# SSM phase tables in short fused instructions, and copies, modulation evictions and a GELU step moved between VectorE and ACT

## The chip, the cores and the metric

The kernel runs on one core of one Trainium2 chip. The metric is the device time of one execution in microseconds (us). The engines are named as in the profile: PE is TensorE (matmul, with its weight loads as PEld), DVE is VectorE, ACT is ScalarE, POOL is GpSimd, and SP only issues DMAs.

## What is computed

Two layers of a diffusion backbone over 512 latent tokens and 256 context tokens, model width 1024. Each layer mixes tokens in three parallel ways that share one input and one output projection, and then has a SwiGLU FFN. Norm and modulation come before each half.

```python
def modulate(x, shift, scale):
    return x * (1 + scale) + shift
...
    h = modulate(rmsnorm(x, g_pre_mix), sh1, sc1) @ w_in
...
    y_ssm, yc_ssm = s5_mixer(u, uc, ...)          # 24 groups, 64 complex states, two directions
    y_fft = fnet_mixer(f, w_fourier)
...
    y_na = na_latent(q, k, v, kc, vc, na_rpb)
    o = jnp.concatenate([y_ssm, y_fft, y_na], axis=-1) @ w_out
...
    x = x + g2 * rmsnorm(swiglu(modulate(rmsnorm(x, g_pre_ffn), sh2, sc2), ...), g_post_ffn)
```

In the S5 mixer the recurrence h = lam_bar * h + B u runs over the tokens, its output passes through a tanh GELU and a GLU. The kernel turns each complex state by a known phase, so that a real scan is left: it needs tables of cos and sin of 2 pi times n times a turn, for n = 0 to 95 steps of eight tokens.

## The kernel before

**Matmuls.** They take float32 split into a high and a low part (`split`, L579: an ACT copy that rounds, then a subtraction for the rest on DVE or POOL), three products each. `wsT` (L584, matmuls at L589) makes the projections `w_in` and gate/up, L1050 is `w_out`, L1146 the down projection.

**Stages.** For each layer: modulation and norm, `make_h` (L537), then `w_in` woven with `ssm` (12 units k: six quadruples of groups u times two directions d), `w_v`, attention woven with FNet and GLU, `w_out` with the second `make_h`, and the FFN, at whose end stands the `make_h` of the next layer. In layer 0 the tables of unit k+1 are made just ahead of their use (`prep_dir` with `jit`, which calls `phase`); those of layer 1 are made during the FFN of layer 0 (`prep`, which calls `phases` and `prep_dir` without `jit`) and loaded back by `tables`. A scheduler that simulates the timeline orders the instructions of each engine when the program is built, so an engine's order is not the order of the source; at run time every engine works its queue in that order.

**The touched places.** `phase` (L395) makes one unit's cos and sin table, 128 partitions x 4 groups x 96: on DVE a product with the turn (through the helper `tt`, L278), an addition of 12582912 that rounds (helper `ts`, L275), and a subtraction (helper `stt`, L281); on ACT Abs (L404) and two Sin (L405, L406). `prep_dir` (L431) makes a unit's matrices: three DVE products into `bm` (L278), three POOL products (L452 to L456), a cleared tile `b0` with 16 of every 32 columns copied (L460, L461), four PE transposes (L464) with an ACT eviction (L469), a small product on PE (L480) whose result DVE copies into `w` (L483, L486). `make_h` transposes the normed rows on PE (L552), evicts with scale and shift by DVE from PSUM (`f`, L275, out c, in b,am,mc) and splits `f` (ACT L580, DVE or POOL L561). `ssm_scan` (L703) has the DVE products, four DVE scans (L724) and the POOL rotation back (L727 to L737). `ssm_out` (L741) ends in the GELU: ACT Square (L758), a DVE `ts`, a DVE `tt`, ACT Tanh (L761), a DVE `stt`.

Of the kernel before, what the change touches and what calls it, by code (L numbers as in the profile page):

```python
# [8 lines left out]
F32 = mybir.dt.float32  # L9
F32R = mybir.dt.float32r  # L10
I32 = mybir.dt.int32
AF = mybir.ActivationFunctionType
ALU = mybir.AluOpType
# [16 lines left out]
TWO_PI = 6.2831845  # L30
# [4 lines left out]
class Builder:  # L35
    def __init__(self, tc, ctx, ap):
        self.tc, self.nc, self.ap = tc, tc.nc, ap
        pool = lambda name, bufs, **k: ctx.enter_context(tc.tile_pool(name=name, bufs=bufs, **k))
        self.ring_raw = pool("ring_raw", 2)
        self.ring_hi = pool("ring_hi", 4)  # L40
        self.ring_lo = pool("ring_lo", 4)
        self.tab_p = pool("tab", 3)
        self.x_p = pool("xp", 3)
        self.g_p = pool("gp", 2)
        self.u_p = pool("up", 1)
        self.s_p = pool("sp", 24)
        self.q_p = pool("qp", 12)
        self.c_p = pool("cp", 22)
        self.z_p = pool("zp", 2)
        self.sm_p = pool("sm", 18)  # L50
        self.ss_p = pool("ss", 12)
        self.am_p = pool("am", 24)
        self.b0_p = pool("b0p", 2)
        self.keep = pool("keep", 1)
        self.ps_p = {t: pool("ps_" + t, n, space=PSUM) for t, n in (("m", 3), ("a", 2), ("t", 2), ("o", 1))}
        self.dr_p = pool("dr", 1, space=DRAM)
# [39 lines left out]
    def consts(self):  # L96
        nc = self.nc
        self.cols = self.k("cols", [128, 8])
        nc.sync.dma_start(self.cols, self.ap["cols"])
        self.ident = self.k("ident", [128, 128])  # L100
        self.nidx = self.k("nidx", [128, 96])
        self.eye16 = self.k("eye16", [128, 16])
        self.junk = self.k("junk", [128, 512], mybir.dt.bfloat16)
        self.zero = self.k("zero", [1, 128], mybir.dt.bfloat16)
        nc.vector.memset(self.zero, 0.0)
        self.sgn, self.nsgn, self.sgn2pi, self.halfpi = (self.cols[:, i:i + 1] for i in range(4))
        self.mhalf = self.cols[:, 4:5]
        self.qd = [self.dram(f"qd{l}", [NH * HD, 2, NT]) for l in range(DEPTH)]
        self.kd = [self.dram(f"kd{l}", [NH * HD, 2, NT]) for l in range(DEPTH)]
        self.ud = [self.dram(f"ud{l}", [G, HC, 8, 128]) for l in range(DEPTH)]  # L110
        self.zd = [self.dram(f"zd{l}", [G, HC, 8, 96]) for l in range(DEPTH)]
        self.tabd = [self.dram(f"tabd{l}", [NU, 2, 128, 1792]) for l in range(DEPTH)]
        self.wd = [self.dram(f"wd{l}", [NU, 128, 240]) for l in range(DEPTH)]
        self.gd = [self.dram(f"gd{l}", [4, DM]) for l in range(DEPTH)]
        self.rbd = [self.dram(f"rbd{l}", [NH, 16, 8, 384]) for l in range(DEPTH)]
        self.xd = [self.dram(f"xd{l}", [6, 128, DM]) for l in range(3)]
        self.turn = [self.k(f"turn{l}", [128, 48]) for l in range(DEPTH)]
        self.rho = [self.k(f"rho{l}", [128, 48]) for l in range(DEPTH)]
        self.mcol = [[self.k(f"mc{l}{a}", [128, 2, 16]) for a in range(3)] for l in range(DEPTH)]
        self.gcol = [self.k(f"gcol{l}", [128, 2, 8]) for l in range(DEPTH)]  # L120
        self.amod = [[self.k(f"am{l}{i}", [128, 2, 8]) for i in range(2)] for l in range(DEPTH)]
        self.dcol = [self.k(f"dcol{l}", [128, NU]) for l in range(DEPTH)]

    def consts_load(self):
        nc = self.nc
        nc.sync.dma_start(self.ident, self.ap["ident"])
        nc.sync.dma_start(self.nidx, self.ap["nidx"])
        nc.sync.dma_start(self.eye16, self.ap["eye16"])
        for l in range(DEPTH):
            nc.sync.dma_start(self.gcol[l], self.ap["gpre"][l])  # L130
            nc.sync.dma_start(self.dcol[l], self.ap["ssm_d"][l])
# [263 lines left out]
    def phase(self, l, u, d, dst):  # L395

        o = (u * 2 + d) * 4
        sh = [128, 4, 96]
        cs, sn = (dst[:, i:i + 384].rearrange("p (g n) -> p g n", g=4) for i in (0, 384))
        self.tt(sn, self.nidx.unsqueeze(1).to_broadcast(sh), self.turn[l][:, o:o + 4].unsqueeze(2).to_broadcast(sh),  # L400
                ALU.mult)
        self.ts(cs, sn, 12582912.0, ALU.add)
        self.stt(sn, cs, -12582912.0, sn, ALU.add, ALU.subtract)
        self.nc.scalar.activation(cs, sn, AF.Abs)  # L404
        self.nc.scalar.activation(cs, cs, AF.Sin, scale=-TWO_PI, bias=self.halfpi)  # L405
        self.nc.scalar.activation(sn, sn, AF.Sin, scale=self.sgn2pi)  # L406

    def phases(self, l, u):

# [20 lines left out]
    def prep_dir(self, l, fin, k, jit, tags):  # L430

        nc = self.nc
        u, d = k // 2, k % 2
        if d == 0:
            self.prep_load(l, u)
        bc, w = self.bc, self.w
        o = k * 4
# [8 lines left out]
        bm, bt = xb[:, 0], xb[:, 1]  # L446
# [4 lines left out]
        g = nc.gpsimd  # L451
# [4 lines left out]
        g.tensor_tensor(out=cl, in0=cl, in1=ct, op=ALU.add)  # L456
        e0 = 1 if d == 0 else 0
        clv = cl[:, :, e0:e0 + 8, :].rearrange("p g e h -> p g (e h)")
        b0 = self.b0_p.tile([128, 4, 32], F32, tag="b0", name="b0")
        nc.vector.memset(b0, 0.0)  # L460
        nc.vector.tensor_copy(b0[:, :, 0:16], bm[:, :, 0 if d == 0 else 7, :])  # L461
        tp = self.ps(tags[0], [128, 4, 128])
        for i in range(4):
            nc.tensor.transpose(tp[:, i, :], bm[:, i].rearrange("p e h -> p (e h)"), self.ident)  # L464
# [13 lines left out]
        kp = self.ps(tags[1], [128, 128])  # L478
# [1 line left out]
            nc.tensor.matmul(kp[32 * i:32 * i + 32, :], b0[:, i, :],  # L480
                             cl[:, i, 1 - e0:9 - e0, :].rearrange("p e h -> p (e h)"), start=True, stop=True)
        if d == 0:
            nc.vector.tensor_copy(w[:, 112:240], kp)  # L483
            self.stt(w[:, 112:128], self.eye16, self.dcol[l][:, u:u + 1], w[:, 112:128], ALU.mult, ALU.add)
        else:
            nc.vector.tensor_copy(w[:, 0:112], kp[:, 0:112])  # L486
            self.tt(w[:, 112:128], w[:, 112:128], kp[:, 112:128], ALU.add)
            nc.sync.dma_start(self.wd[l][u], w)
            if jit:
                res.append(self.toeplitz(l, u))  # L490
# [47 lines left out]
    def make_h(self, l, i, xn, t0, ks=range(8)):  # L538

        nc = self.nc  # L540
# [8 lines left out]
        for k in ks:  # L549
# [2 lines left out]
                nc.tensor.transpose(tp[:, j, :], xn[j][k // 4][:, k % 4 * 128:(k % 4 + 1) * 128], self.ident)  # L552
            a, s = self.amod[l][i][:, v, k:k + 1], self.modB(l, i, v, k)
            f = self.c()
            self.ts(f, tp.rearrange("p j c -> p (j c)"), a, ALU.mult, s, ALU.add)
            ins = self.split(self.hh[k][v][:, cs], self.hl[k][v][:, cs], f, nc.gpsimd if k % 2 else nc.vector)
            if t0 == 0:
                self.h_ins = ins
# [181 lines left out]
    def ssm_out(self, l, k, tab, hh):  # L740
# [14 lines left out]
            self.z = self.z_p.tile([128, 8, 96], F32, tag="z", name="z")  # L755
        z = self.z
        w3 = self.q(shape=(128, 4, 96))
        nc.scalar.activation(w3, yp, AF.Square)  # L758
        self.ts(w3, w3, 0.044715, ALU.mult, 1.0, ALU.add)
        self.tt(w3, w3, yp, ALU.mult)  # L760
        nc.scalar.activation(w3, w3, AF.Tanh, scale=0.7978845608028654)  # L761
        o = (u % 2) * 4
        self.stt(z[:, o:o + 4, :], w3, 1.0, yp, ALU.add, ALU.mult)
# [545 lines left out]
def _consts():  # L1309
    f = np.float32  # L1310
    c = {}
    c["ident"] = np.eye(128, dtype=f)
    sg = np.where(np.arange(128) < 64, 1.0, -1.0)
    cols = np.zeros((128, 8))
    cols[:, 0], cols[:, 1], cols[:, 2], cols[:, 3], cols[:, 4] = sg, -sg, sg * TWO_PI, np.pi / 2, -0.5
    c["cols"] = cols.astype(f)
    c["nidx"] = np.broadcast_to(np.arange(96, dtype=f), (128, 96)).copy()
    p = np.arange(128)
# [94 lines left out]
```

## Time and profile before

| what | value |
|---|---|
| three runs, median (lowest to highest) | 1692.61 us (1690.66 to 1693.28) |
| the profiled execution, its own time | 1691.85 us |
| its span, first to last instruction | 1690.1 us |
| mean granted TensorE clock | 0.978 of full speed |
| busy: PE / DVE / ACT / POOL | 1613.3 / 1038.1 / 611.8 / 381.3 us |
| DMA | 242.96 MB, mean 144 GB/s |

Busy time of an engine is the time in which at least one of its instructions runs; an instruction that is held up by another engine counts as busy. A window row gives this by stretch. A group row gives the mean of one instruction, and after the bar the idle time of the engine before the group and what ended it.

### The profile page before, as it was taken

Reading aid. Unit: us, or ns where it says so; the run is one execution under the profiler, and the core shown is the slowest. Engines: PE = TensorE matmul, PEld = TensorE weight load, DVE = VectorE, ACT = ScalarE, POOL = GpSimd, SP = SyncE. Lnnn points to the kernel's source line nnn. Section 1 sums busy time; section 2 is a strip of 40 time slices with the busy share of each in tenths; the row PEclk is TensorE's granted clock in tenths of the full one; section 3 lists DMA queues with packets and bytes.
Section 4 is the critical chain, followed back from the end, with each engine's and each line's share of the span. In section 5 each row is a group of like instructions: output and inputs, shape, how many; then the busy total and the mean of one; then the engine's idle time right before and its main releaser. Section 6 shows DMA issues by size and latency. Waiting matters only on the chain. (4 is left out here: it accounts for less than half of the span.)

```text
span 1690.1 us, 23611 instructions
## 1 busy us (share of the span) xinstructions
PE 1613.3 (95%) x9121; PEld 1320.7 (78%) x9121; DVE 1038.1 (61%) x1893; ACT 611.8 (36%) x1091; POOL 381.3 (23%) x384
## 2 busy tenths in 40 slices
PE   5987789999999999999999999999999999999997
PEld 1776676678898888878878787988877888888886
DVE  7799984675774657534433348698773634454455
ACT  5433344572636522212211126421563532222222
POOL 3367673200320224100000005267410200000002
PEclk8999799999999999999999999999999999999999
DMA  9343338652403433544242527478714422222222
GB/s 327 126 133 115 113 101 278 213 214 102 169 32 119 165 116 118 181 156 150 103 155 105 203 84 241 133 242 248 228 45 143 157 100 100 75 100 100 100 75 87
DMA packets 101681, 242.96 MB, mean 144 GB/s; under 512 B 25457, under 2 KB 56817, under 8 KB 88257
## 3 DMA queue, kind: packets, MB, share of 16 engines
q1 hardware_dynamic: 98256, 232.80, 40.4%
q0 software_dynamic: 3312, 8.65, 1.7%
q8 instruction: 72, 1.18, 0.3%
q14 instruction: 41, 0.33, 0.1%
HBM read 204.12 MB, written 38.47 MB: 144 GB/s over the span
## 5 line engine op out<-in xcount | busy, mean ns | idle before, releaser
L589 PE MATMUL b<-s,wh 128*128 128x512 f32 (+1 forms) x1856 | 553.0, 376 | 1.7 <-DVE s L561 1.3
L589 PEld LDWEIGHTS b<-s,wh 128*128 128x128 f32 x1856 | 339.6, 190 | 73.9 <-issue 10.6
L589 PE MATMUL b<-s,wl 128*128 128x512 f32 (+1 forms) x928 | 346.6, 375 | 1.9 <-DVE wl L561 1.9
L580 ACT ACTIVATE wh<-wr 128x1024 fp32r<-128x1024 f32 (+1 forms) x188 | 190.3, 1034 | 334.2 <-PE b L589 232.1
L561 DVE TENSOR_TENSOR wl<-wr,wh 128x1024 fp32r<-128x1024 f32 (+1 forms) x188 | 231.8, 1247 | 108.8 <-ACT wh L580 103.4
L278 DVE TENSOR_TENSOR q<-q,b 128x512 f32<-128x512 f32 (+1 forms) x192 | 129.2, 676 | 165.8 <-PE b L1146 165.1
L589 PEld LDWEIGHTS b<-s,wl 128*128 128x128 f32 x928 | 175.7, 190 | 32.5 <-DVE wl L561 3.0
L589 PE MATMUL b<-c,wh 128*128 128x256 f32 x944 | 184.8, 290 | 0.0
L589 PEld LDWEIGHTS b<-c,wh 128*128 128x128 f32 x944 | 155.7, 196 | 5.9 <-issue 0.6
L281 DVE SCALAR_TENSOR_TENSOR s<-s,b 128x512 f32<-128x512 f32 x88 | 60.2, 684 | 132.9 <-PE b L589 83.8
L1146 PE MATMUL b<-wh,tab 128*128 128x512 f32 x400 | 137.2, 393 | 0.7 <-DVE q L278 0.7
L589 PE MATMUL b<-c,wl 128*128 128x256 f32 x472 | 135.2, 289 | 0.0
L1146 PE MATMUL b<-wh,s 128*128 128x512 f32 x384 | 129.6, 391 | 0.0
L1178 POOL TENSOR_TENSOR q<-q,g 128x512 f32<-128x512 f32 x10 | 13.8, 1382 | 360.6 <-ACT junk L515 360.6
L589 PEld LDWEIGHTS b<-c,wl 128*128 128x128 f32 x472 | 92.8, 197 | 1.7 <-issue 0.4
L1146 PEld LDWEIGHTS b<-wh,tab 128*128 128x128 f32 x400 | 75.1, 188 | 20.0 <-ACT c L1123 2.5
L1146 PEld LDWEIGHTS b<-wh,s 128*128 128x128 f32 x384 | 72.1, 188 | 20.0 <-issue 2.5
L1146 PE MATMUL b<-wl,tab 128*128 128x512 f32 x200 | 78.3, 392 | 0.0
L527 POOL TENSOR_TENSOR ss<-ss,cols 128x1 f32<-128x1 f32 x42 | 31.0, 737 | 194.1 <-DVE ss L281 193.4
L1146 PE MATMUL b<-wl,s 128*128 128x512 f32 x192 | 74.6, 390 | 0.0
L452 POOL TENSOR_TENSOR u<-x,u 128x576 f32<-128x576 f32 x24 | 31.5, 1311 | 168.8 <-PE b L480 143.3
L580 ACT ACTIVATE s<-s 128x512 fp32r<-128x512 f32 x36 | 22.6, 627 | 113.6 <-DVE s L281 58.4
(301 smaller groups left out, 2761.7 us busy)
## 6 DMA issues: line engine op xcount, KB each, us to landing
wr<-in_w_gu SPq DMA_DIRECT2D x44, 1024.0 KB
wmod<-in_w_mod SPq DMA_DIRECT2D x46, 512.0 KB
wr<-in_w_down SPq DMA_DIRECT2D x22, 1024.0 KB
wmod<-in_w_mod SPq DMA_DIRECT2D x16, 1024.0 KB
wr<-in_w_in SPq DMA_DIRECT2D x10, 1024.0 KB
u<-in_w_mod SPq DMA_DIRECT2D x18, 512.0 KB
wr<-in_w_out SPq DMA_DIRECT2D x8, 1024.0 KB
tab<-tabd SPq DMA_DIRECT2D x12, 640.0 KB
```

Of the source, the lines that this page charges most:

```text
L278: self.nc.vector.tensor_tensor(out=out, in0=a, in1=b, op=op)
L281: self.nc.vector.scalar_tensor_tensor(out=out, in0=a, scalar=s, in1=b, op0=op0, op1=op1)
L452: g.tensor_tensor(out=cl, in0=v(2).unsqueeze(2).to_broadcast(sc), in1=clr.unsqueeze(3).to_broadcast(sc), op=ALU.mult)
L527: nc.gpsimd.tensor_tensor(out=ss[:, 3:4], in0=ss[:, 2:3], in1=self.mhalf, op=ALU.pow)
L561: (eng or self.nc.vector).tensor_tensor(out=lo, in0=x, in1=hi.bitcast(F32), op=ALU.subtract)
L580: ins = self.nc.scalar.activation(hi, x, AF.Copy)
L589: self.nc.tensor.matmul(out, a[k], h[k][v][:, cs], start=(k == 0 and i == 0), stop=(k == 7 and i == 2))
L1146: nc.tensor.matmul(pd, a[v][:, cs], w[:, ds], start=(j == 0 and i == 0), stop=(j == n - 1 and i == 2))
L1178: (nc.gpsimd, nc.vector)[hf].tensor_tensor(out=oo[hf], in0=oo[hf], in1=gates[t // 4][:, hf * 512:(hf + 1) * 512], op=ALU.mult)
```

## The change

`phase`: the three DVE instructions of 384 columns become four fused `ts` of 96 columns (index times turn plus 12582912, the turn as a per-partition operand), an ACT pass that takes 12582912 off again (Identity with a bias column), and four `stt` of 96 columns (index times turn minus the rounded value). The sign of the result is reversed, so the sine takes the reversed scale column. `phases`, used for layer 1, stays as it is.

`prep_dir`: `b0` becomes two lasting tiles, cleared once by POOL at the start; the copy into it and the copies of the small product go from DVE to ACT.

`make_h`: the eviction `f` goes from DVE to ACT, with scale and shift as per-partition operands.

`ssm_out`: the factor 0.044715 goes into the Square's scale, and `ts` and `tt` become one `stt`.

```diff
+        self.b0 = [self.k(f"b0{i}", [128, 4, 32]) for i in range(2)]
...
-        self.mhalf = self.cols[:, 4:5]
+        self.mhalf, self.nsgn2pi, self.nmagic = (self.cols[:, i:i + 1] for i in range(4, 7))
...
+        for b0 in self.b0:
+            nc.gpsimd.memset(b0, 0.0)
...
-        sh = [128, 4, 96]
         cs, sn = (dst[:, i:i + 384].rearrange("p (g n) -> p g n", g=4) for i in (0, 384))
-        self.tt(sn, self.nidx.unsqueeze(1).to_broadcast(sh), self.turn[l][:, o:o + 4].unsqueeze(2).to_broadcast(sh),
-                ALU.mult)
-        self.ts(cs, sn, 12582912.0, ALU.add)
-        self.stt(sn, cs, -12582912.0, sn, ALU.add, ALU.subtract)
+        turn = [self.turn[l][:, o + g:o + g + 1] for g in range(4)]
+        for g in range(4):
+            self.ts(cs[:, g, :], self.nidx, turn[g], ALU.mult, 12582912.0, ALU.add)
+        self.nc.scalar.activation(cs, cs, AF.Identity, bias=self.nmagic)
+        for g in range(4):
+            self.stt(sn[:, g, :], self.nidx, turn[g], cs[:, g, :], ALU.mult, ALU.subtract)
         self.nc.scalar.activation(cs, sn, AF.Abs)
         self.nc.scalar.activation(cs, cs, AF.Sin, scale=-TWO_PI, bias=self.halfpi)
-        self.nc.scalar.activation(sn, sn, AF.Sin, scale=self.sgn2pi)
+        self.nc.scalar.activation(sn, sn, AF.Sin, scale=self.nsgn2pi)
...
-        b0 = self.b0_p.tile([128, 4, 32], F32, tag="b0", name="b0")
-        nc.vector.memset(b0, 0.0)
-        nc.vector.tensor_copy(b0[:, :, 0:16], bm[:, :, 0 if d == 0 else 7, :])
+        b0 = self.b0[k % 2]
+        nc.scalar.activation(b0[:, :, 0:16], bm[:, :, 0 if d == 0 else 7, :], AF.Copy)
...
-            nc.vector.tensor_copy(w[:, 112:240], kp)
+            nc.scalar.activation(w[:, 112:240], kp, AF.Copy)
...
-            nc.vector.tensor_copy(w[:, 0:112], kp[:, 0:112])
+            nc.scalar.activation(w[:, 0:112], kp[:, 0:112], AF.Copy)
...
-            self.ts(f, tp.rearrange("p j c -> p (j c)"), a, ALU.mult, s, ALU.add)
+            nc.scalar.activation(f, tp.rearrange("p j c -> p (j c)"), AF.Identity, scale=a, bias=s)
...
-        nc.scalar.activation(w3, yp, AF.Square)
-        self.ts(w3, w3, 0.044715, ALU.mult, 1.0, ALU.add)
-        self.tt(w3, w3, yp, ALU.mult)
+        nc.scalar.activation(w3, yp, AF.Square, scale=0.044715 ** 0.5)
+        self.stt(w3, w3, 1.0, yp, ALU.add, ALU.mult)
```

## Rows read from the trace of the kernel before

**Rows 1.** Windows: start:end, length; PE, PEld, DVE, ACT, POOL busy; clock, DMA.
```profile
28.00:50.00 22.00, 15.63 (x66) 6.80 (x67) 21.28 (x46) 10.58 (x23) 14.79 (x10) 0.73 0.89 324
97.00:241.00 144.00, 112.88 (x693) 98.42 (x692) 143.35 (x231) 57.79 (x100) 106.79 (x89) 0.88 0.33 101
241.00:1666.00 1425.00, 1411.57 (x7929) 1160.51 (x7929) 806.27 (x1425) 502.82 (x885) 233.37 (x256) 0.99 0.42 143
```

**Rows 2.** Waits of PE, 97 to 241: total us, times, longest.
```profile
PE b L480 <- POOL u L456: 11.2, 2, 6.8
...
PE b L746 <- DVE z L281: 0.4, 1, 0.4
```

**Rows 3.** Waits of PE, 0 to 97.
```profile
PE b L552 <- DVE c L275: 6.1, 2, 3.8
```

**Rows 4.** Timeline, 41 to 50: start, length, instruction, [idle before].
```profile
42.34 0.42 ACT L580 ACTIVATE s<-c 128x256 fp32r<-128x256 f32 x1 [5.16 <-DVE c L275]
...
48.50 0.69 PE L552 MATMUL b<-ident,s 128*128 128x128 f32 x2 [3.80 <-DVE c L275]
```

**Rows 5.** Groups by form, DVE, 97 to 241: busy us, mean ns, idle before.
```profile
L278 DVE TENSOR_TENSOR tab<-nidx,turn 128x384 f32<-128x384 f32 x9 | 9.5, 1058 | 0.0
...
L281 DVE SCALAR_TENSOR_TENSOR tab<-tab 128x384 f32<-128x384 f32 x10 | 8.8, 879 | 0.1
L275 DVE TENSOR_SCALAR tab<-tab 128x384 f32<-128x384 f32 x10 | 6.8, 681 | 0.0
...
L461 DVE COPY b<-x 128x64 f32<-128x64 f32 x10 | 6.2, 616 | 0.0
...
L275 DVE TENSOR_SCALAR q<-q 128x384 f32<-128x384 f32 x4 | 2.2, 548 | 0.0
...
L460 DVE MEMSET b<- 128x128 f32 x9 | 1.5, 165 | 0.0
L483 DVE COPY x<-b 128x128 f32<-128x128 f32 x5 | 1.4, 284 | 0.1
```

**Rows 6.** Timeline of DVE and POOL, 130 to 160.
```profile
130.26 4.34 POOL L727 TENSOR_TENSOR q<-q,tab 128x384 f32<-128x384 f32 x1 [2.71 <-DVE q L724]
131.22 0.35 DVE L275 TENSOR_SCALAR tab<-tab 128x384 f32<-128x384 f32 x1
...
134.57 0.55 DVE L281 SCALAR_TENSOR_TENSOR tab<-tab 128x384 f32<-128x384 f32 x1
...
141.91 1.68 POOL L688 TENSOR_TENSOR s<-s 128x512 f32<-128x512 f32 x1
...
142.73 1.08 DVE L275 TENSOR_SCALAR tab<-tab 128x384 f32<-128x384 f32 x1
...
158.13 0.49 DVE L278 TENSOR_TENSOR tab<-nidx,turn 128x384 f32<-128x384 f32 x1
158.54 0.18 DVE L461 COPY b<-x 128x64 f32<-128x64 f32 x1
158.63 1.09 DVE L724 TENSOR_TENSOR_SCAN q<-rho,q 128x96 f32<-128x96 f32 x4
```

**Rows 7.** Groups by form, DVE, whole run.
```profile
L275 DVE TENSOR_SCALAR c<-b,am,mc 128x256 f32<-128x256 f32 x88 | 45.5, 537 | 22.3 <-PE b L552 21.8
...
L275 DVE TENSOR_SCALAR sm<-sm 128x48 f32<-128x48 f32 x46 | 8.3, 187 | 1.1
...
L281 DVE SCALAR_TENSOR_TENSOR sm<-sm 128x48 f32<-128x48 f32 x18 | 3.7, 208 | 0.6
L275 DVE TENSOR_SCALAR q<-q,am 128x256 f32<-128x256 f32 x12 | 3.7, 350 | 0.2
```

**Rows 8.** Groups by form, ACT, 97 to 241.
```profile
L405 ACT ACTIVATE tab<-tab,cols 128x384 f32<-128x384 f32 x10 | 6.2, 615 | 0.2
...
L404 ACT ACTIVATE tab<-tab 128x384 f32<-128x384 f32 x10 | 5.2, 524 | 44.7 <-DVE tab L281 44.7
...
L694 ACT ACTIVATE c<-b 128x256 f32<-128x256 f32 x5 | 1.8, 365 | 2.9 <-PE b L589 2.9
```

More of the change, by code (lines that the diff above doesn't have):

```diff
@@ L52, in __init__ @@
         self.am_p = pool("am", 24)
-        self.b0_p = pool("b0p", 2)
         self.keep = pool("keep", 1)
@@ L1315, in _consts @@
     cols[:, 0], cols[:, 1], cols[:, 2], cols[:, 3], cols[:, 4] = sg, -sg, sg * TWO_PI, np.pi / 2, -0.5
+    cols[:, 5], cols[:, 6] = -sg * TWO_PI, -12582912.0
     c["cols"] = cols.astype(f)
```

## The prediction, as put on record before the changed kernel ran

> **What bounds the kernel now.** I read the table of windows first, because PE is busy 95% of the span and a share over the whole run says little. From 241 to 1666 us PE is busy 1411.57 of 1425 us [rows 1]: whatever the change takes off DVE or ACT there can be worth at most the 13.4 us of gaps. The tail after 1666 is not touched. So the change is decided in two early stretches. From 28 to 50 us PE is busy 15.63 of 22, and DVE 21.28 [rows 1]. From 97 to 241 us, the SSM stage of layer 0, DVE is busy 143.35 of 144 while PE works 112.88, with a mean granted clock of 0.88 [rows 1]. The waits of PE in this stage are six groups, from 11.2 us for a POOL product down to 0.4 us [rows 2], and no single one explains its 31 us of idle time: PE is late because the unit chain runs through a full DVE.
>
> The second thing to see is what "busy" means for DVE here. The same instruction has two lengths. The `ts` of `phase` takes 0.35 us at 131.22 and 1.08 us at 142.73 [rows 6]; the latter began while a POOL instruction ran from 141.91 to 143.59, and ended at 143.81, just after it. The four scans of 96 columns at 158.63 took 1.09 us together [rows 6]; POOL's next work waits for such scans, idle (2.71 us before 130.26). So an instruction of DVE that works in SBUF alone stands still until the POOL instruction ahead of it has ended, and POOL is busy 106.79 of the 144 us [rows 1]. In the groups, this makes 1058, 879 and 681 ns of what takes 490, 550 and 350 alone [rows 5, 6].
>
> This is also what the Trainium skill says (SBUF — State Buffer, "SBUF: two separate sides"): DVE and GpSimd share a port pair under an exclusive lock, held for the whole instruction. By that rule a stall belongs to the POOL instruction, not to the DVE one that meets it, and the sum of the stage would stay near zero, as it does below from rows alone.
>
> **SSM stage of layer 0, DVE.** One unit loses: product 0.49, `ts` 0.35, `stt` 0.55, copy into b0 0.18 [rows 6], clearing 0.165, copy of the small product 0.284 [rows 5], and half a GELU `ts` (one per two units; same shape as the phase `ts`, 0.35) 0.18. That is 2.20 us of lone time. Neighbours overlap by about 0.08 us (158.13 + 0.49 = 158.62, the next starts at 158.54 [rows 6]), so 6.5 instructions free 2.20 - 0.52 = 1.68 us. It gains four `ts` and four `stt` of 96 columns. A `ts` lies between 187 ns at 48 columns [rows 7] and 350 at 384 [rows 6]: 210 at 96, plus a per-partition operand, for which the 350 ns at 256 columns [rows 7] against 288 on the same line give 60: 0.27 us. A `stt` lies between 208 at 48 [rows 7] and 550 at 384: 257, plus 60: 0.32. Sum 4 x 0.27 + 4 x 0.32 = 2.36, less 8 x 0.08: 1.72 us. **Without stalls the change is +0.04 us per unit, +0.5 us over the 11 units in the stage.** The small-product copy and the clearing do not meet POOL (0.28 and 0.165 us with no long form), so part of their 0.29 us per unit may come back as a longer stall elsewhere: up to 3.2 us. I take +2 us.
>
> Then the stalls. On average the four SBUF instructions removed lose 0.57, 0.33, 0.33 and 0.44 us (means less lone times) [rows 5, 6], and that can go three ways: it stays, because POOL's instructions are the same and the next SBUF instruction of DVE meets them (0 us); it goes with the removed instructions and the short ones meet nothing, 1.67 + 0.10 for the GELU step = 1.77 us per unit, -19 us; or each of the eight short ones also meets a POOL instruction, 8 x 0.42 - 1.77 = +1.6 us per unit, +18 us. I take 0, because DVE never idles in the stage and POOL's work is unchanged: a stall that one instruction escapes waits for the next.
>
> **SSM stage, ACT and the new wait.** ACT gains per unit one Identity with a bias column (0.615, as the Sin with a column [rows 8]), a b0 copy of 64 columns and a small-product copy (each under the 0.365 of 256 columns from PSUM [rows 8]): about 1.2 us, 13 us on 57.79 of 144 [rows 1]. ACT has the room. The Identity is a new turn DVE to ACT to DVE: the four `stt` wait for it, behind them in DVE's queue stand the products and scans of the unit before, and for those POOL and PE wait. If the scheduler puts other DVE work between, it costs nothing; if not, 0.6 us and a handover per unit, about 0.8 x 11 = 9 us, and more where ACT's queue is itself held up, as in its 44.7 us of waits for the phase `stt` [rows 8]. The copies into b0 and w add like hops, PE's small product behind the one, DVE's last step on w behind the other; they are hidden as long as ACT is free. I take 0 here.
>
> **Start, 28 to 50 us.** Part of the first `make_h` lies here, and each of its `f` is 537 ns [rows 7] of a DVE that is full. PE waits 6.1 us in two waits for them [rows 3], the longer 3.80 us up to 48.50, while ACT had sat idle 5.16 us before 42.34 [rows 4]. On ACT an `f` should take 0.365 plus two columns at 0.09 (615 against 524 [rows 8]) = 0.55 us, the same as on DVE, and the split's copy follows it on the same engine. Behind the `f` in PE's queue stand modulation matmuls and the first `w_in`, so an earlier `f` moves all that follows. Ends: -6.1 us (both waits go) and +2 us (an `f` queued on ACT behind a norm that waits for POOL). I take 60% of the waits: -3.6 us.
>
> **The rest.** The other 64 `f`, at the ends of `w_out` and of the FFN, change engine at the same price where PE has nearly no gaps; the layer-1 copies and six GELU steps lie in stages where PE is nearly full. All together I take -0.5 us, with -4 and +4 as ends (part of the 13.4 us of gaps [rows 1]; a longer ACT queue before the first gate/up). The two extra POOL clears at the start stand against idle POOL time: nothing.
>
> **Sum.** -3.6 + 2 + 0 - 0.5 = -2.1 us on the profiled 1691.85 us (span 1690.1 and 1.75 us around it), 1689.7; on the median of 1692.61, 1690.5. **Forecast 1690 us.**
>
> **The rivals.** (B) *The stalls go.* For it: the POOL instruction of 4.34 us at 130.26 [rows 6], through which DVE kept running, so eight short ones in two rows might pass in one go. Against: POOL comes in turn at 142.73 [rows 6], and the long means of all four forms [rows 5] say that this is the common case. Full price -19 - 3.6 - 0.5: 1669; half of it, 1678. (C) *More instructions, more stalls.* It decides if a POOL instruction is pending at most of the eight boundaries: +18 in full, 1691.85 + 18 + 0.5 - 4.1 = 1706; half of it, 1697. The Trainium skill speaks for this side (VectorE: DVE Perf Modes, "Rules for kernel authors"): minimise the number of DVE operations rather than fuse, as each pays its own fixed time; the 187 ns of a 48-column `ts` beside 350 for eight times the columns agree. (D) *The Identity's turn shows*, in the SSM stage of layer 0, from the point where DVE's queue has the `stt` next: 9 us to 13 us, 1691.85 - 2.1 + 9 to 13: 1699 to 1703. (E) *The start gains nothing*, as PE then waits for ACT: 1693.
>
> **How the numbers follow.** Forecast case with E 0.52 (1685 to 1695), B 0.20, C 0.13, D 0.15. About 0.2%, 3.4 us, is what a measurement of this kernel can tell from no change. Faster than 1689.2: all of B and 0.22 of the forecast case, 0.42. Within: 0.30 and 0.02 of the mild ends of C and D, 0.32. Slower: 0.26. The range leaves out the full price of B and the worst of C and D, a tenth on either side: 1674 to 1706.
>
> **What the changed profile would show.** Right: the stretch up to DVE's saturation ends some 3 to 4 us earlier and the L552 waits of PE at the start are gone; the SSM stage keeps its length within 4 us, DVE still over 98% busy there, with the remaining SBUF instructions (x<-x,u and the like) longer on average. B: these keep their length and the stage is 10 us shorter or more. C: the 96-column instructions average over 0.5 us. D: DVE shows idle time released by ACT in that stage. Wrong outright would be a reordered queue that opens gaps after 241 us.

## The result, and the profile after

The changed kernel takes 1710.28 us (median of four runs, 1708.78 to 1715.85) against 1692.38 us for the kernel before on the same chip: a ratio of 1.0113, 95% interval 1.0088 to 1.0138. It is 17.9 us slower where 2.6 us faster was forecast, and lies outside the range.

The windows of the changed kernel (start:end, length; PE, PEld, DVE, ACT, POOL busy; clock, DMA) answer to [rows 1]:

```profile
28.00:50.00 22.00, 15.41 (x71) 7.30 (x73) 17.44 (x42) 15.94 (x36) 14.52 (x10) 0.70 0.84 301
97.00:241.00 144.00, 113.62 (x676) 97.85 (x675) 142.73 (x237) 63.31 (x124) 98.03 (x86) 0.87 0.32 99
241.00:1666.00 1425.00, 1403.88 (x7865) 1150.37 (x7865) 765.06 (x1312) 535.37 (x971) 232.87 (x260) 1.00 0.42 143
```

The SSM stage of layer 0 looks as before: DVE full, PE at 113.62 us. It is the long stretch after it, in which PE was busy 1411.57 us, that has 7.7 us more of gaps. DVE has 41 us less to do there, and the time did not fall for it.

The queues are ordered anew, so equal times hold different work. To find the places, I weighted each PE instruction of both traces with one length per form (that of the form in the kernel before) and asked when each kernel had done the same sum of PE work. A delay taken in this way is good to a few tenths of a us, at 241 us to about 1 us. The windows between such points:

Kernel before:

```profile
60.00:241.00 181.00, 149.88 (x971) 132.75 (x969) 170.67 (x282) 73.28 (x129) 117.12 (x99) 0.90 0.34 106
241.00:380.00 139.00, 138.15 (x966) 97.03 (x966) 82.91 (x197) 72.58 (x161) 33.58 (x46) 0.98 0.70 231
1070.00:1250.00 180.00, 175.87 (x1138) 152.45 (x1136) 142.49 (x280) 71.57 (x141) 89.84 (x101) 0.97 0.61 193
1300.00:1340.00 40.00, 37.92 (x253) 33.85 (x253) 25.52 (x48) 23.14 (x52) 10.90 (x16) 1.00 0.45 159
```

Changed kernel, the same PE work:

```profile
58.20:242.90 184.70, 153.88 (x974) 135.06 (x973) 167.59 (x288) 88.88 (x173) 110.68 (x96) 0.90 0.34 109
242.90:385.30 142.40, 140.02 (x964) 97.17 (x963) 84.11 (x194) 74.19 (x162) 34.48 (x49) 1.00 0.68 225
1075.90:1264.00 188.10, 177.20 (x1138) 153.51 (x1137) 139.20 (x269) 75.13 (x148) 88.65 (x101) 0.97 0.59 185
1313.90:1356.90 43.00, 40.20 (x257) 34.51 (x256) 18.62 (x33) 30.56 (x69) 10.93 (x16) 1.00 0.40 147
```

So the profiled execution (span 1706.9 us, 16.8 more than before) is made of: start -1.8; SSM stage of layer 0 +3.7; attention of layer 0 +3.4; the long FFN part +0.6; SSM stage and attention of layer 1 (1070 to 1250) +8.1; end of `w_out` of layer 1 (1300 to 1340) +3.0. Of the three largest after 241 us, attention of layer 0 holds no edited instruction, the SSM stage of layer 1 its six GELU steps and six `f`, the end of `w_out` 16 of the 88 `f`.

The waits of PE in the changed kernel, 97 to 241 (total us, times, longest), answer to [rows 2]:

```profile
PE b L466 <- DVE x L280: 17.0, 8, 5.2
PE b L482 <- POOL u L459: 4.1, 2, 2.6
```

The first is the wait of PE's transposes for the DVE products of `prep_dir`. It is now more than half of PE's 30.4 us of idle time; in the kernel before it was:

```profile
PE b L464 <- DVE x L278: 8.9, 3, 4.5
```

From 0 to 97, answering to [rows 3] (`f` is now L557, on ACT):

```profile
PE b L554 <- ACT c L557: 5.2, 2, 4.7
```

From 1075.9 to 1264, SSM stage and attention of layer 1:

```profile
PE b L751 <- POOL q L739: 4.6, 2, 2.5
PE b L716 <- DMA u<-tabd: 2.8, 1, 2.8
PE b L716 <- DMA tab<-tabd: 2.3, 2, 1.8
```

Groups by form of DVE, 97 to 241 (busy us, mean ns, idle before), answering to [rows 5]:

```profile
L283 DVE SCALAR_TENSOR_TENSOR tab<-nidx,turn,tab 128x96 f32<-128x96 f32 x36 | 22.4, 681 | 0.0
L726 DVE TENSOR_TENSOR_SCAN q<-rho,q 128x96 f32<-128x96 f32 x40 | 21.7, 601 | 0.0
L280 DVE TENSOR_TENSOR x<-x,u 128x512 f32<-128x512 f32 x18 | 20.2, 1150 | 0.1
...
L277 DVE TENSOR_SCALAR tab<-nidx,turn 128x96 f32<-128x96 f32 x36 | 11.1, 359 | 0.1
```

For nine units the short instructions take 33.5 us; the three long ones took 25.1 us for nine to ten [rows 5]. The scans and the products of `prep_dir` had taken, in the kernel before:

```profile
L278 DVE TENSOR_TENSOR x<-x,u 128x512 f32<-128x512 f32 x20 | 24.9, 1273 | 0.0
L724 DVE TENSOR_TENSOR_SCAN q<-rho,q 128x96 f32<-128x96 f32 x41 | 12.2, 355 | 0.0
```

Groups by form of ACT, whole run, answering to [rows 7], where `f` on DVE takes 537 ns:

```profile
L557 ACT ACTIVATE c<-b,mc,am 128x256 f32<-128x256 f32 x88 | 47.5, 560 | 25.1 <-PE b L554 24.3 <-DVE am L283 0.5
```

and 97 to 241, answering to [rows 8]: the new Identity and the Abs behind it, for which ACT sat idle 44.7 us before.

```profile
L404 ACT ACTIVATE tab<-tab,cols 128x384 f32<-128x384 f32 x9 | 5.5, 612 | 14.3 <-DVE tab L277 10.0 <-DVE x L280 4.2
...
L407 ACT ACTIVATE tab<-tab 128x384 f32<-128x384 f32 x9 | 4.7, 524 | 26.8 <-DVE tab L283 26.8
```

### The profile page after: what moved, and what is told of

It is laid out like the page before. It is cut to its first block, busy times and chain, and to the rows that moved or that the text cites. A ratio compares the mean times of both kernels' runs of the same rounds, so it can differ in the third digit from the quotient of the medians.

```text
span 1706.9 us, 23697 instructions
## 1 busy us (share of the span) xinstructions
PE 1623.5 (95%) x9121; PEld 1324.7 (78%) x9121; DVE 992.8 (58%) x1781; ACT 669.8 (39%) x1239; POOL 370.5 (22%) x386
## 5 line engine op out<-in xcount | busy, mean ns | idle before, releaser
L591 PEld LDWEIGHTS b<-s,wh 128*128 128x128 f32 x1856 | 338.8, 190 | 75.6 <-issue 10.8
L280 DVE TENSOR_TENSOR q<-q,b 128x512 f32<-128x512 f32 x180 | 122.7, 684 | 165.3 <-PE b L1147 164.7
L591 PEld LDWEIGHTS b<-s,wl 128*128 128x128 f32 x928 | 175.8, 190 | 30.4 <-DVE wl L563 0.4
L1124 ACT ACTIVATE s<-b 128x512 f32<-128x512 f32 x44 | 25.9, 589 | 82.7 <-PE b L591 82.7
```

The costliest lines, as they stand in the source:

```text
L280: self.nc.vector.tensor_tensor(out=out, in0=a, in1=b, op=op)
L591: self.nc.tensor.matmul(out, a[k], h[k][v][:, cs], start=(k == 0 and i == 0), stop=(k == 7 and i == 2))
L1124: nc.scalar.activation(tmp[v], gp, AF.Tanh, scale=0.5)
```

## The experiments

All kernels compute the whole of the two layers. Medians are of runs on one chip, beside the kernel before (whose medians lie between 1691.7 and 1692.4). "Late" is the delay of the profiled execution at equal PE work, at the point that before reaches at that time. One execution scatters. Up to 420 us a1 and b4 run the same instructions in the same order on every engine, as do the changed kernel and b3, and c3 and d3; at 380 us they differ by 3.5 to 3.8 us. So "late" tells places, where several kernels agree, and medians tell prices.

| run | median us | ratio, 95% interval | late at 60 | 241 | 380 | 1070 | 1250 | 1340 us |
|---|---|---|---|---|---|---|---|---|
| changed kernel | 1710.28 | 1.0113, 1.0088 to 1.0138 | -1.8 | +1.9 | +5.3 | +5.9 | +14.0 | +16.9 |
| a1 make_h alone | 1692.01 | 0.9995, 0.9981 to 1.0010 | -2.8 | -9.1 | -7.8 | -5.9 | -5.6 | -2.6 |
| a2 phase alone | 1695.87 | 1.0021, 1.0012 to 1.0029 | +0.6 | -0.2 | +4.0 | +4.4 | +5.4 | +5.3 |
| a3 copies alone | 1693.82 | 1.0011, 1.0000 to 1.0022 | +0.2 | +0.2 | +1.5 | +1.6 | +1.4 | +1.3 |
| a4 GELU alone | 1698.00 | 1.0035, 1.0021 to 1.0048 | +0.6 | -3.2 | -1.6 | -1.6 | +5.8 | +5.7 |
| b1 changed, POOL order, layer 1 | 1706.11 | 1.0085, 1.0071 to 1.0098 | -2.4 | +2.2 | +5.5 | +7.5 | +10.8 | +13.8 |
| b2 changed, POOL order, both | 1701.31 | 1.0061, 1.0049 to 1.0074 | -1.1 | +3.7 | +2.9 | +3.6 | +9.9 | +12.8 |
| b3 changed, f on ACT at start only | 1708.76 | 1.0095, 1.0080 to 1.0111 | -1.7 | +3.0 | +8.8 | +8.7 | +17.2 | +17.1 |
| b4 before, f on ACT at start only | 1688.20 | 0.9980, 0.9968 to 0.9991 | -2.5 | -6.1 | -4.0 | -4.0 | -3.2 | -3.4 |
| c1 GELU alone, POOL order | 1697.53 | 1.0031, 1.0018 to 1.0043 | -0.7 | -4.4 | +0.9 | +0.8 | +5.9 | +5.8 |
| c2 b4 and GELU, POOL order | 1690.09 | 0.9992, 0.9983 to 1.0001 | -2.4 | -4.1 | -6.0 | -5.6 | -3.3 | -3.4 |
| c3 b2 without phase | 1692.65 | 1.0005, 0.9992 to 1.0018 | -2.9 | -9.3 | -6.8 | -4.1 | +0.2 | +3.2 |
| c4 b2, f on ACT at start only | 1697.40 | 1.0030, 1.0021 to 1.0039 | -1.8 | +2.9 | +2.0 | +2.3 | +7.1 | +7.0 |
| d1 the turn of phase alone | 1691.93 | 0.9994, 0.9981 to 1.0006 | +1.2 | -2.6 | -1.1 | -1.3 | +1.4 | +1.3 |
| d2 b2, GELU edit in layer 0 only | 1699.12 | 1.0041, 1.0027 to 1.0054 | -1.6 | +3.0 | +2.2 | +4.1 | +4.3 | +7.2 |
| d3 see below | 1685.27 | 0.9954, 0.9936 to 0.9972 | -2.4 | -11.1 | -10.6 | -10.5 | -10.0 | -10.1 |
| d4 d3 without copies | 1689.55 | 0.9982, 0.9971 to 0.9993 | -3.0 | -4.7 | -6.7 | -6.2 | -3.6 | -3.5 |
| e1 d3 with phase | 1694.75 | 1.0015, 1.0004 to 1.0026 | -1.9 | +2.7 | +1.8 | +1.9 | +3.3 | +3.2 |
| e2 d3, POOL free | 1684.41 | 0.9952, 0.9940 to 0.9965 | -2.8 | -9.0 | -9.7 | -9.5 | -8.2 | -8.3 |

**One part at a time (a1 to a4).** Each is the kernel before with one group of hunks of the diff above. The theory named "order" was that the edited instructions cost nearly nothing and that the newly ordered queues make the loss.

```diff
 a1, make_h
-            self.ts(f, tp.rearrange("p j c -> p (j c)"), a, ALU.mult, s, ALU.add)
+            nc.scalar.activation(f, tp.rearrange("p j c -> p (j c)"), AF.Identity, scale=a, bias=s)
 a2, phase: its hunk (four ts, Identity on ACT, four stt), the two columns
 a3, prep_dir
-        nc.vector.tensor_copy(b0[:, :, 0:16], bm[:, :, 0 if d == 0 else 7, :])
+        nc.scalar.activation(b0[:, :, 0:16], bm[:, :, 0 if d == 0 else 7, :], AF.Copy)
 ... and the two copies of kp; b0 kept
 a4, ssm_out
-        self.ts(w3, w3, 0.044715, ALU.mult, 1.0, ALU.add)
-        self.tt(w3, w3, yp, ALU.mult)
+        self.stt(w3, w3, 1.0, yp, ALU.add, ALU.mult)
```

> Only the edit of make_h: the 88 evictions f on ACT, all else as before. Theory 'order' (the edited instructions cost almost nothing; the scheduler, which orders every queue by its own simulated clock, puts other work elsewhere in a different order and that opens gaps after 241 us): the loss of 17.9 us is not in this edit by price; this kernel lies within 4 us of before at the start (28 to 50 us gains 2 to 4 us), and any further difference sits in stretches that hold no make_h. Theory 'ACT eviction' (an f on ACT stands behind other ACT work at the ends of w_out and of the FFN, where PE waits for it): 10 us to 18 us slower than before, the loss at the ends of w_out and FFN of both layers.

> Only the edit of phase: eight instructions of 96 columns and an ACT pass in the place of three of 384. Theory 'order': the SSM stage of layer 0 keeps its length within 4 us; what differs from before by more sits after 241 us, in stages that run no phase at all, and may be up to 10 us of either sign. Theory 'short instructions' (each fixed time and each lock of the shared port is paid): 8 us to 18 us slower, all of it in the SSM stage of layer 0.

> Only the edits of prep_dir: b0 kept and cleared once, its copy and the copies of the small product on ACT. Theory 'order': SSM stage of layer 0 within 4 us of before, differences after 241 us of either sign up to 10 us. Theory 'copy turn' (PE's small product waits for a copy that stands in ACT's queue): 3 us to 10 us slower, in the SSM stages of layer 0 and layer 1 (about 100 to 240 us and 1090 to 1200 us), with waits of PE for ACT there.

> Only the edit of ssm_out: one step less on DVE per GELU, 12 in all, no engine changed. By its price alone -0.35 us x 12 = 4.2 us of DVE work, at most 2 us of the end. Theory 'order': a difference of more than 3 us of either sign even from this, placed after 241 us in stages without a GELU. The other theories: within 2 us of before, nothing after 241 us but in the SSM stage of layer 1.

Measured: 0, +3.9, +1.9 and +6.0 us, 11.9 together, so 6 us of the loss belong to no part alone. The GELU edit, which only takes work off DVE, loses 7.4 us between 1070 and 1250. That is the size that "order" expected of it, but not the place: the stretch holds the GELU steps of layer 1. `make_h` gains 8 us until 1030 and gives back 2 us at the end of the FFN and 3 us at the end of `w_out` of layer 1: two of the places of "ACT eviction", at less than its price. `phase` comes in under the 8 to 18 us of "short instructions", and its loss shows only between 241 and 380 us, in attention, as "order" had it. Yet its chain of units is late before that: the last `stt` of `phase` ends at 245.2 us where it ended at 234.5.

**POOL's order (b1, b2).** POOL works its queue in order. In the SSM stage of layer 1, before, the last subtraction of unit 9 (L735 to L737) stands ahead of the products of unit 10 (L727 on). Timeline of POOL, kernel before (start, length, instruction, [idle before]):

```profile
1176.76 1.22 POOL L729 TENSOR_TENSOR q<-q,tab 64x384 f32<-64x384 f32 x1
1178.04 0.10 POOL L735 MEMSET q<- 128x4 f32 x1
1178.10 0.88 POOL L736 TENSOR_TENSOR q<-q 128x256 f32<-128x256 f32 x1
1178.94 0.49 POOL L737 TENSOR_TENSOR q<-q 128x124 f32<-128x124 f32 x1
...
1180.04 1.01 POOL L727 TENSOR_TENSOR q<-q,tab 128x384 f32<-128x384 f32 x1
```

Changed kernel (two lines further on): unit 10's product comes first, and it has to wait.

```profile
1185.47 1.23 POOL L731 TENSOR_TENSOR q<-q,tab 64x384 f32<-64x384 f32 x1
1187.89 1.02 POOL L729 TENSOR_TENSOR q<-q,tab 128x384 f32<-128x384 f32 x1 [1.19 <-PE b L751]
1188.99 1.01 POOL L730 TENSOR_TENSOR q<-q,tab 64x384 f32<-64x384 f32 x1
1189.94 0.11 POOL L737 MEMSET q<- 128x4 f32 x1
...
1190.81 0.45 POOL L739 TENSOR_TENSOR q<-q 128x124 f32<-128x124 f32 x1
```

From the end of L729 (L731) to the end of unit 9's subtraction it is 1.45 us before and 4.56 us after. What follows is a chain: PE's product, ACT's Square, and DVE's GELU step, behind which unit 11's scan stands. DVE sat idle for that step 7.25 us in the changed kernel:

```profile
1196.50 0.56 DVE L283 SCALAR_TENSOR_TENSOR q<-q,b 128x384 f32<-128x384 f32 x1 [7.25 <-ACT q L760]
```

and 4.07 us in the kernel before:

```profile
1185.31 0.36 DVE L275 TENSOR_SCALAR q<-q 128x384 f32<-128x384 f32 x1 [4.07 <-ACT q L758]
```

In the order of the queues every kernel with the GELU edit in layer 1 has this swap there, the one with that edit alone too, unless POOL's order is held; none of the others has. b1 and b2 hold it by an edge between two instructions of the same engine, which is no wait:

```diff
-        gp.tensor_tensor(out=t1, in0=gg, in1=co, op=ALU.mult)
+        prev = self.gp_last if l == 1 and k else None   # b2: if k
+        with self.tc.issue_after(prev) if prev is not None else ExitStack():
+            gp.tensor_tensor(out=t1, in0=gg, in1=co, op=ALU.mult)
 ... the other POOL instructions of ssm_scan inside, then
+        self.gp_last = getattr(end, "ins", end)
```

> The changed kernel with the same instructions; only the order of POOL's queue in the SSM stage of layer 1 is fixed: the products of a unit stand behind the last subtraction of the unit before it (in the changed kernel, and in the kernel with the GELU edit alone, those of unit 10 stand ahead of the subtraction of unit 9; in the kernel before they don't). Theory 'order': 4 us to 8 us faster than the changed kernel's 1710.3, so 1702 to 1706, with the gain between 1170 and 1240 us. Rival 'the layer-1 loss is the price of the edited instructions or of the fuller ACT queue': within 2 us of 1710.

> As the last, with the order of POOL's queue fixed in the SSM stages of both layers (layer 0 has the same swap of units 9 and 10). Theory 'order': the gain of the last run, and in layer 0 a further 0 to 5 us by the end of attention (about 380 us), 1698 to 1706. Rival 'price': within 2 us of 1710.

4.2 us come back with layer 1 held and 9.0 us with both, both as "order" expected, with not one instruction changed. So half of the loss is order: shown for the changed kernel. That it is POOL's order alone is not shown, as the edge lets other queues move too (in the trace of b2 some 70 of DVE's 1781 instructions stand elsewhere). In layer 0 the gain lies in attention: the three kernels with the changed kernel's queues there (changed, b1, b3) lose 3.3 to 5.8 us between 241 and 380, the four with the same instructions and POOL held (b2, c4, d2, e1) gain 0.8 or 0.9. It is not a rule: with the GELU edit alone the kernel with POOL free (a4) loses 1.6 us there, the one with POOL held (c1) 5.3.

**make_h at the start only (b3, b4).**

```diff
+            if l == 0 and i == 0:
+                nc.scalar.activation(f, tp.rearrange("p j c -> p (j c)"), AF.Identity, scale=a, bias=s)
+            else:
                 self.ts(f, tp.rearrange("p j c -> p (j c)"), a, ALU.mult, s, ALU.add)
```

> The changed kernel, with f of make_h back on DVE except for the first make_h (layer 0, ahead of the first w_in). Theory 'ACT queue at the end of w_out': the 3.0 us that the changed kernel loses between 1310 and 1325 us come back, as they were also lost with make_h alone, and 0 to 2 us at 1040 to 1070; 1705 to 1707. Rival 'order only': a difference of either sign elsewhere and none there.

> The kernel before, with f of make_h on ACT in the first make_h alone. Start 2.5 us to 3 us earlier, as with make_h alone. Theory 'ACT queue at the end of w_out': the gain of 8 us that make_h alone still had at 1030 us is kept to the end, 1683 to 1687, faster than both kernels. Rival: the gain in the SSM stage of layer 0 came from the order of a particular build and does not come again, 1689 to 1692.

The pair a1 and b4 shows the end of `w_out`. Windows of the same PE work, between the points that the kernel before reaches at 1310 and 1340; a1:

```profile
1304.30:1337.40 33.10, 30.95 (x214) 27.78 (x213) 14.10 (x24) 24.86 (x55) 9.28 (x13) 0.95 0.45 166
```

b4:

```profile
1306.60:1336.60 30.00, 27.90 (x209) 25.59 (x208) 20.95 (x39) 17.49 (x38) 9.25 (x13) 1.00 0.50 184
```

With the `f` on ACT, ACT works 24.9 of 33.1 us, in one queue with the norm's sums and the splits; with `f` on DVE both engines have room and the stretch is 3.1 us shorter. The granted clock differs in this pair (0.95 and 1.00), but the changed kernel loses its 3.0 us at 1.00. Where it loses them ACT is nearly full (14.57 of 16 us), and PE, as busy as before, gets through 100 matmuls where the kernel before did 117. Changed kernel:

```profile
1330.80:1346.80 16.00, 14.73 (x100) 12.27 (x99) 9.99 (x14) 14.57 (x31) 6.15 (x8) 1.00 0.43 154
```

Kernel before, 13.8 us earlier:

```profile
1317.00:1333.00 16.00, 14.83 (x117) 14.02 (x117) 12.39 (x19) 9.83 (x20) 4.98 (x7) 1.00 0.62 222
```

The table bears it out: between 1250 and 1340 the six kernels with these `f` on ACT lose 2.9 or 3.0 us each, the other kernels nothing (within 0.2). b4 is faster than before, by 3.5 us where 5 to 9 were expected: at 380 us it has 4.0 us of the gain where a1, with the same queues, had 7.8. b3 missed. In b3 the 3 us come back too, but it is 3.5 us later by 380, and the median gains only 1.5 us, which the intervals can't tell from nothing. Its queues are those of the changed kernel until 440 us, so this is not order but the scatter of one execution.

**Mixtures (c1 to c4).** Same edits, combined.

> The GELU edit alone (1698.0 us without more), with the order of POOL's queue held in both SSM stages, units one after the other. Theory 'order': the whole loss of the GELU edit is the swap of units 9 and 10, so the time comes back to that of the kernel before or under it, 1689 to 1693. Rival 'the fused step on DVE costs by itself': stays at 1696 to 1699.

> The kernel before with the two edits that should be good: f on ACT in the first make_h alone (1688.2 us by itself) and the GELU edit with POOL's order held. Theory 'order': 1684 to 1689, under both kernels. Rival: any further edit moves the queues again and the gain of the start is lost, 1690 to 1696.

> The changed kernel without the edit of phase, POOL's order held (with phase: 1701.3 us). Theory 'phase costs 4 us in the SSM stage of layer 0, as alone': 1696 to 1698, with the gain ahead of 250 us. Rival 'what is left of the loss sits in the copies, or in the mixture': 1700 to 1703.

> The changed kernel with f on ACT in the first make_h alone and POOL's order held (with all f on ACT: 1701.3 us). Theory 'ACT queue at the end of w_out': 1697 to 1700, the 3 us between 1310 and 1325 us gone. Rival 'order elsewhere eats it', as in the changed kernel without POOL's order, where attention of layer 0 took 3 us more: 1700 to 1704.

c1 missed: with POOL held the GELU edit alone still costs 5.5 us, and falls into the range of its rival "the fused step on DVE costs by itself". The trace speaks against that rival: the step takes 0.56 us in place of 0.36 and 0.55, and in the SSM stage of layer 0, where a4 and c1 have it too, they gain 3.8 and 3.7 us. PE's waits in layer 1 are now mostly for DMAs (4.4 us, and 2.5 for POOL). In SP's queue the edit has also moved a 1 MB weight load (L569, in_dft) ahead of eight stores of z and the table of a unit behind them. Timeline of SP, changed kernel, which has the same order there:

```profile
1153.02 0.38 SPq L569 DMA_DIRECT2D wr<-in_dft  x1
1153.50 5.27 SPq L767 DMA_DIRECT2D zd<-z  x8
1158.87 0.38 SPq L509 DMA_DIRECT2D tab<-tabd  x1
```

Kernel before: the same stores and the same table, 3.83 us for the stores; the weight load comes behind them, at 1157.01.

```profile
1147.15 3.83 SPq L766 DMA_DIRECT2D zd<-z  x8
1151.10 0.38 SPq L507 DMA_DIRECT2D tab<-tabd  x1
```

c2, at 1690.1 us, fell into its rival's range: 2.3 us of its gain go between 1070 and 1250, where it has the same order. c3 missed both expectations, on the good side: without the edit of `phase` the time falls by 8.7 us, twice what it cost alone. c4 came as expected: `f` on ACT outside the start costs 3.9 us.

**What phase costs, and the rest of layer 1 (d1 to d4, e1, e2).**

```diff
 d1, on the kernel before
         self.ts(cs, sn, 12582912.0, ALU.add)
-        self.stt(sn, cs, -12582912.0, sn, ALU.add, ALU.subtract)
+        self.nc.scalar.activation(cs, cs, AF.Identity, bias=self.nmagic)
+        self.tt(sn, cs, sn, ALU.subtract)
 d2, on b2
+        if l == 0:
+            (Square with scale, one stt)
+        else:
+            (Square, ts, tt)
 d3: f on ACT at the start only, copies on ACT, GELU as in d2, POOL held; phase as before
 d4: d3 without the prep_dir hunks;  e1: d3 with the phase hunk;  e2: d3 without the POOL edge
```

> The kernel before, with only the turn of phase: the product, the addition of 12582912 and the last subtraction stay three DVE instructions of 384 columns, but 12582912 is taken off on ACT between them. Theory 'short instructions' (phase's loss of 3.9 us alone, 8.6 us in the mixture, comes from eight DVE instructions in the place of three, which meet POOL's instructions one by one): within 2 us of before, 1690 to 1694. Theory 'turn' (DVE waits for ACT's pass, or later work waits behind it): as phase alone or worse, 1695 to 1705, with the loss ahead of 250 us.

> The changed kernel, with the GELU edit in layer 0 alone (layer 1 has the old steps, six more DVE instructions of 0.35 us) and POOL's order held. In SP's queue of layer 1 the weight load then stands behind the table of unit 8 again, as in the kernel before. With the GELU edit in both layers and POOL held: 1701.3 us. Theory 'SP order': 1695 to 1698, the loss between 1150 and 1240 us falls from 7 us to 0 to 3 us. Rival 'the fused step is worth its 2 us and the loss is elsewhere': 1701 to 1704.

> No edit of phase; make_h on ACT in the first make_h alone, copies on ACT, GELU edit in layer 0 alone, POOL's order held. If the parts add up as the runs before say (gain of 7 us by 380 us, as without phase, and no loss in layer 1): 1683 to 1687, faster than both kernels. Rival 'each build's order is a lot of its own': 1688 to 1695.

> As the last without the edits of prep_dir (copies stay on DVE). Copies alone cost 1.9 us: if parts add, 1 to 2 us faster than the last, 1682 to 1686; with the GELU edit also in layer 1 it took 1690.1 us. Rival: 1688 to 1695.

> The fastest kernel so far (1685.3 us: f on ACT in the first make_h alone, copies on ACT, GELU edit in layer 0, POOL's order held) with the edit of phase put in. If the short instructions cost what they cost in the mixture: 1692 to 1696, the loss ahead of 250 us. If only what they cost alone: 1688 to 1690.

> The fastest kernel so far without the edge that holds POOL's order: in layer 0 the products of unit 10 then stand ahead of the last subtraction of unit 9. If that swap costs what it did in the changed kernel's layer 0: 1687 to 1690. If not: 1684 to 1686.

d1, as "short instructions" expected: the turn through ACT is free, so `phase` costs by its eight DVE instructions. Their number, length and operands change together, and no run parts these. The timeline of the changed kernel shows two parts of the price. Alone, four `ts` and four `stt` of 96 columns with POOL idle (DVE) take 1.80 us together:

```profile
206.53 0.80 DVE L277 TENSOR_SCALAR tab<-nidx,turn 128x96 f32<-128x96 f32 x4
...
209.39 1.00 DVE L283 SCALAR_TENSOR_TENSOR tab<-nidx,turn,tab 128x96 f32<-128x96 f32 x4
```

and `stt` beside POOL's rotation (DVE and POOL; it answers to [rows 6]):

```profile
131.36 1.71 POOL L729 TENSOR_TENSOR q<-q,tab 128x384 f32<-128x384 f32 x1 [3.76 <-DVE q L726]
132.12 3.35 DVE L283 SCALAR_TENSOR_TENSOR tab<-nidx,turn,tab 128x96 f32<-128x96 f32 x4
133.15 1.15 POOL L730 TENSOR_TENSOR q<-q,tab 64x384 f32<-64x384 f32 x1
134.35 1.01 POOL L731 TENSOR_TENSOR q<-q,tab 64x384 f32<-64x384 f32 x1
```

The four short instructions last over three POOL instructions: they end at 135.47, L731 at 135.36. Between two POOL instructions one of them passes, now and then two. All `ts` and `stt` of the stage, duration min/median/max:

```profile
L277 DVE TENSOR_SCALAR tab<-nidx,turn x36: 238/261/1403, 113.7 to 233.4; 128x96 f32<-128x96 f32 x36
...
L283 DVE SCALAR_TENSOR_TENSOR tab<-nidx,turn,tab x36: 283/480/1467, 116.2 to 236.4; 128x96 f32<-128x96 f32 x36
```

Seven of nine groups of four `stt` take 1.92 to 3.35 us in place of 1.00; most `ts` pass unharmed. The place in the queue accounts for most of this, not the form. By the start and end of each instruction in this trace, 29 of the 36 `ts` ran while POOL stood idle, and none of these took over 272 ns; of the seven beside POOL, four took 1.0 to 1.4 us. Of the `stt` 27 ran beside POOL, and 18 of them took 0.64 us or more. Five of the seven slow groups begin less than 1.7 us after the scans end, when POOL, which had waited for the scans, begins or has begun its rotation. The one group of `ts` that stands right behind scans is held as well:

```profile
223.19 2.31 DVE L277 TENSOR_SCALAR tab<-nidx,turn 128x96 f32<-128x96 f32 x4
```

The pair e1 and d3 differs in the edit of `phase` alone; the SSM stage in e1:

```profile
97.00:241.00 144.00, 114.33 (x672) 98.07 (x671) 142.79 (x237) 63.17 (x124) 98.50 (x86) 0.86 0.32 99
```

and in d3:

```profile
97.00:241.00 144.00, 118.90 (x756) 105.39 (x755) 136.16 (x205) 63.65 (x123) 113.06 (x99) 0.92 0.34 102
```

Without the short instructions PE does 84 matmuls more in the same 144 us and DVE has 7.8 us of idle time. The price of the edit of `phase` is 9.5 us here, as e1 expected from the mixture, and 8.7 us between b2 and c3.

d2: with the old GELU steps in layer 1, which cost DVE six instructions more, the delay between 1070 and 1250 is 0.2 us (6.3 in b2). Over all kernels, those with the GELU edit in layer 1 and POOL's order free lose 7.4 to 8.5 us there, with POOL held 2.3 to 6.3, and those without the edit there -0.2 to 2.7. So the rest of layer 1's loss came with the GELU edit there, whose instructions are cheaper; order is what is left to explain it, and in d2 the weight load stands behind the table again. Which queue weighed most is not shown. The median gains only 2.2 us (2.7 from c4 to e1): at 1699.1 us d2 missed both expected ranges. d3, with the parts that proved good, takes 1685.27 us as expected, faster than both kernels. d4 missed its expectation and fell into the rival's: the copies on ACT cost 1.9 us alone, but without them d3 is 4.3 us slower. e2: POOL's edge isn't needed once layer 1 has its old order; the swap in layer 0 that came back costs nothing here.

Taken down one by one, the changed kernel's loss goes: 1710.3, POOL's order 1701.3 (b2), GELU edit out of layer 1 1699.1 (d2), `f` on ACT only at the start 1694.8 (e1), `phase` as before 1685.3 (d3).

## Why the prediction was wrong, point by point

**What bounds the kernel.** Right as far as it went: the SSM stage of layer 0 stays bound by DVE (142.73 of 144 us). Wrong in what it was used for: PE busy 1411.57 of 1425 us [rows 1] was read as a cap on gains, and I let it stand as a cap on losses too. Between 1070 and 1250, where PE had been busy 175.87 of 180 us, its gaps grew from 4.1 to 10.9 us.

**Phase, price alone.** Estimated 4 x 0.27 + 4 x 0.32 us less overlap = 1.72; four `ts` in a row take 0.80 and four `stt` 1.00, so 1.80. Right.

**Phase, stalls: right as a sum, by a reason that failed.** "I take 0, because DVE never idles in the stage and POOL's work is unchanged: a stall that one instruction escapes waits for the next." For `phase` itself the stalls grew. By the means, the three long instructions took 1.06 + 0.88 + 0.68 = 2.62 us per unit [rows 5], 1.23 more than alone (1.39); the eight short ones take 4 x 0.36 + 4 x 0.68 = 4.16 us, 1.87 more than alone (4 x 0.26 + 4 x 0.31 = 2.29 with POOL idle). What made the sum come out near 0 is that the copy and the GELU step went with stalls of 0.44 and 0.10 us: 1.23 + 0.54 = 1.77 against 1.87. And the stalls did not pass to the next instructions as a rule: the products x<-x,u became shorter (1273 to 1150 ns), against the sign that the prediction gave, the scans longer (355 to 601).

Rival C had a chance of 0.13. Its mark came true, a mean over 0.5 us for the 96-column instructions ((359 + 681) / 2 is 520 ns), its price did not: the short ones stall by about half of its 8 x 0.42 us, which no more than pays for the stalls that went. That its half price, 9 us for the whole stage, equals the price of `phase` in the mixtures is chance. The Trainium skill's rule that I had set beside C (VectorE: DVE Perf Modes, "Rules for kernel authors": minimise the number of operations, don't fuse for speed) is what the price of `phase` bears out: a `stt` with a quarter of the columns takes 0.25 us alone where a quarter of 0.55 would be 0.14, and 0.84 us beside POOL in the group at 132.12.

**Why the stage came out at +3.7 us** (+2 predicted): two terms of opposite sign, each taken too small. By the prediction's own terms `phase` costs 1.72 - (1.39 - 3 x 0.08) = 0.57 us per unit, 6.3 us over 11 units, with no stalls added; the mixtures give 9.5 and 8.7 us. The copies and the GELU step were to bring 5.8 us, less 1.5 for longer stalls; c3 and d3, which have them, the new start and POOL's order held, gain 6.4 and 8.7 us between 60 and 241. A sum that was nearly right, in part by luck. So start and stage hold 3.5 us of an error of about 20: at 241 us the changed kernel is 1.9 us late where -1.6 was taken.

**The Identity's turn.** 0 us taken, 0.9994 measured in d1. Right: DVE has other work in between, and ACT, not DVE, does the waiting. Its price was 612 ns for the 615 taken.

**Start.** -3.6 us taken; -1.8 us in the changed kernel, -2.5 us with 3.5 us at the end in b4. The sign is right, the size half to two thirds, and the reason failed: the waits for `f`, which were to go, hardly shrank (6.1 us [rows 3] to 5.2 us). DVE's load in 28 to 50 us fell from 21.28 to 17.44 us; that this made the start earlier is not shown.

**The rest: the step that failed.** "All together I take -0.5 us, with -4 and +4 as ends", for layer 1's GELU steps and the other 64 `f`. Measured after 241 us: +15.0 us, of which +8.1 in 1070 to 1250, +3.4 in attention of layer 0 and +3.0 at `w_out`. The term priced the edited instructions and took the order of the queues as given. With edges that hold POOL's order, and not an instruction changed, 9.0 us come back (b2); the GELU steps of layer 1, which take work off DVE, cost 2.2 us more (d2). The +3.0 at `w_out` is the "longer ACT queue" that the prediction had as an end: 560 ns against 537 is the price of an `f`, and says nothing of ACT's load there, 30.56 us in the stretch for 23.14 before. "Wrong outright would be a reordered queue that opens gaps after 241 us" names the event, and no rival was given a chance for it.

**Open.** Why `phase` costs 3.9 us alone and 9 us in the mixtures, although its chain of units is later by 10.7 us alone and by 6.5 us from d3 to e1 (last `stt` at 236.7 for 230.2); why the copies change sign; why attention of layer 0 moves with POOL's order, and not always the same way; what in layer 1 the GELU edit still costs with POOL's order held. The runs show the sizes, not the causes.

## What to carry to other kernels

When a scheduler orders the queues from its own simulated times, an edit need not be local: cost the edited instructions, then give a chance of its own to a reordered queue in every stage with little slack, and look first at the queues that run in order behind one late step (POOL, SP). On DVE count instructions before columns, the more so beside a busy POOL: eight of 96 columns took 4.16 us per unit where three of 384 took 2.62. Look also at where they stand: right behind the instruction that POOL waits for, they meet its work. Move an eviction only where the receiving engine is idle: the same edit was worth 3.5 us at the start and cost 3 us at `w_out`.

## What was not expected of the hardware

Four `stt` of 96 columns take 1.00 us alone and 3.35 us beside three POOL products of 1.0 to 1.7 us, each of which lets one or two through. `ts` of the same shape with one tile operand look unharmed (median 261 ns), but only because 29 of 36 ran while POOL stood idle; four that did not took 1.0 to 1.4 us. That DVE and GpSimd hold each other off for a whole instruction stands in the Trainium skill (SBUF — State Buffer, "SBUF: two separate sides"); it names DVE instructions with two SBUF inputs and those in a two-port mode. The `stt`, which read two tiles, agree (0.64 to 1.47 us for 18 of the 27 that ran beside POOL, 0.31 with POOL idle). The `ts` read one tile and a column and are held too; by which of the two conditions, no run here shows.
